# An account of every engine's clock in place of fixed waits: emission order in a two-layer hybrid decoder trunk

## The chip, the cores and the metric

The kernel runs on one core of one Trainium2 chip. The metric is the device time of one execution in microseconds (us), here the median of three runs. The engines are TensorE (PE, matrix products and transposes), VectorE (DVE), ScalarE (ACT), GpSimd (POOL) and SyncE (SP), whose queue issues nearly all transfers.

## The reference

The kernel computes two layers of a decoder trunk on 512 tokens of 1024 features, all in float32:

```python
for l in range(DEPTH):
    proj = rms_norm(h, norm_mix_pre[l]) @ w_in[l]
    (aq, ak, av, cb, cc, cx, gq, gk, gv, ga, gb, gg) = jnp.split(proj, split_idx, axis=-1)
    y_attn = dilated_attention_mixer(aq, ak, av, cos, sin)          # 4 heads of 64
    y_conv = short_conv_mixer(cb, cc, cx, conv_short[l])            # 256 channels
    y_gdn = gated_deltanet_mixer(gq, gk, gv, ga, gb, gg, ...)       # 4 heads of 128, chunked recurrence
    mix = jnp.concatenate([y_attn, y_conv, y_gdn], axis=-1) @ w_out[l]
    h = h + rms_norm(mix, norm_mix_post[l])
    xa = memory_cross_attention(rms_norm(h, norm_xattn_pre[l]), rms_norm(mem, norm_mem[l]), w_xq[l], w_xkv[l], w_xo[l])
    h = h + rms_norm(xa, norm_xattn_post[l])
    gate, up = jnp.split(rms_norm(h, norm_ffn_pre[l]) @ w_gate_up[l], 2, axis=-1)
    h = h + rms_norm((jax.nn.silu(gate) * up) @ w_down[l], norm_ffn_post[l])
```

The DeltaNet solves a triangular system per chunk and head, and carries a state from chunk to chunk; the kernel uses chunks of 128 tokens, four in all.

## The kernel before

**Bulk products.** The weight projections are products of float32 accuracy made of parts: each weight chunk (512 KB) is loaded into a raw tile, split by ACT into a rounded part `hi` (name ending in `_hi`) and by DVE into the rest `lo`, and each block takes three products (`mm3`, lines 207 to 209). The names are those of the columns: gk, gq, gv and gg (DeltaNet keys, queries, values, gate), aq and av (attention; ak is part of aq), cb and cx (convolution), wo (output projection), xk, xv, xq and xo (cross-attention), gu (feed-forward's gate and up), da and db (the halves of its down projection). A number behind the name is the token block (wo, xo, db) or column block.

**Dependent chains.** Between them stand small chains: a norm ahead of each sub-layer (`prenorm`: squares and sums on ACT, a power on POOL, the scaling on DVE into `mix_hn`, `xa_hn` or `ff_hn`, transposes on PE into `mix_pt`, `xa_pt` or `ff_pt`, and their split into `hT..._h` on ACT and `hT..._l` on DVE); the same for the memory (`mem_x`, `mem_pt`, `mT`); the norm and residual behind an output projection (`wo_z`, `wo_sq`, `wo0p_r`, then `h`; in the feed-forward `dacc`, `fsq`, `ffnp_r`); and the DeltaNet's chain. That one makes the decays: a product gives their running sums by columns and by rows (`dcol`, `drow`), DVE copies them (`dcol_s`, `drow_s`), SP stores drow_s to DRAM (`dD`) and loads it back on all partitions (`edrow`), ACT makes `relT` of it, and for each chunk DVE forms `A` from relT and the product `G` of the keys (`gk_c`). A goes through DRAM into a substitution and its inverse through DRAM again (`X`, `Z` from `dX`, `dZ`), then through products (`W1p`, `dZ`) to the recurrence. `fq` is a factor for the queries, from the sum of squares `gq_ss` by a power on POOL (`gq_r`).

**What sets the order.** All is one program that is emitted by tasks. A task is a Python generator; it emits some instructions and yields a wait in ns or the name of an event. `Driver.run` always continues the ready task of the lowest priority number; the bulk has 50, chains have less. `Driver.t` counts PE's time by fixed numbers, and a clock each for DVE and ACT says only when what they were given is done. A chain that needs PE yields `lag(extra)`: until DVE and ACT are through, 300 ns, and an extra that is set by hand for each place:

```python
        yield self.lag({"mix": 3000, "xa": 7000, "ff": 2500}[name])
```

`chunk(i)`, called by the bulk, loads up to chunk i + 3 and splits up to i + 2 at that moment. What is emitted is a priority: the framework then lists the instructions by it and by their dependences, and each engine runs its own list in order. Tiles come from rings of fixed numbers of buffers: 3 raw tiles, 5 each of hi and lo, and in the accumulator memory 3 banks for bulk, 3 ("g") and 2 ("a") for chains.

Nearly all instructions of DVE and ACT are recorded at line 122 (the helper `Engine`), transposes at 201, float32 products at 197, and POOL's powers at 228 and 595.

Of the kernel before, what the change touches and what calls it, by code (L numbers as in the profile page):

```python
# [26 lines left out]
# SBUF tiles of 2 KB, by stream: slots of a stream are given out in the order of emission  # L27
# [6 lines left out]
def shape_constants():  # L34
    """Identity, triangles, block and window masks, rotary frequencies: all from shapes alone."""
# [18 lines left out]
class Driver:  # L54
# [5 lines left out]
    def __init__(self):  # L60
        self.t = 0.0
        self.tasks = []
        self.events = {}
        self.n = 0
        self.engines = {"v": 0.0, "a": 0.0}

    def busy(self, engine, ns):
        self.engines[engine] = max(self.engines[engine], self.t) + ns
# [9 lines left out]
    def fire(self, event):  # L78
        self.events[event] = self.t + self.lag()

    def ready(self, task):
        if task[4] is not None:
            if task[4] not in self.events:
                return None
            task[3] = max(task[3], self.events[task[4]])
            task[4] = None
        return task[3]
# [22 lines left out]
class Engine:  # L110
    """An engine whose instructions are also counted on the driver's clock."""

    def __init__(self, engine, driver, name, fixed, per):
        self._e, self._d, self._n, self._f, self._p = engine, driver, name, fixed, per

    def __getattr__(self, op):
        f = getattr(self._e, op)

        def call(*args, **kw):
            n = max(math.prod(x.shape[1:]) for x in list(args) + list(kw.values()) if hasattr(x, "shape"))  # L120
            self._d.busy(self._n, self._f + self._p * n)
            return f(*args, **kw)  # L122
        return call


class Group:
    """One projection: columns of a weight against activations, feature- or token-major."""
# [22 lines left out]
class Trunk:  # L150
    AHEAD = 2

    def __init__(self, ctx, tc, T, out, dbg=None):
        self.tc, self.nc, self.T, self.out = tc, tc.nc, T, out
# [3 lines left out]
        self.raw_p = pool("raw", 3)  # L158
        self.w_p = pool("w", 5)
# [5 lines left out]
        self.dr = Driver()  # L165
        self.lag = self.dr.lag
        self.v = Engine(tc.nc.vector, self.dr, "v", 140, 1.0)
        self.a = Engine(tc.nc.scalar, self.dr, "a", 200, 0.83)
        self.groups = []
        self.loaded = []  # L170
        self.made = []

    def B(self, tag, name, shape=(128, 512), dt=F32):
        return self.b_p.tile(list(shape), dt, tag="b" + tag, name=name, bufs=SLOTS[tag])

    def T8(self, name, shape=(128, 4, 512), dt=F32):
        return self.t8_p.tile(list(shape), dt, tag="t8", name=name)

    def sm(self, name, w=16):
        return self.s_p.tile([128, w], F32, tag="sm%d" % w, name=name, bufs={32: 2, 16: 26}.get(w, 20))  # L180

    def ps(self, tag, name, shape=(128, 512)):
        return self.ps_p.tile(list(shape), F32, tag="ps" + tag, name=name, bufs=BANKS[tag])
# [5 lines left out]
    @staticmethod  # L189
    def later(wait, gen):  # L190
        yield wait
        yield from gen

# [1 line left out]
    def mm(self, out, a, b, start=True, stop=True):  # L195
        """float32 product of up to 128 columns."""
        self.nc.tensor.matmul(out, a, b, start=start, stop=stop)  # L197
        self.dr.t += 215.0 * max(128, out.shape[-1]) / 128

    def tr(self, out, src):  # L200
        self.nc.tensor.transpose(out, src, self.ident)  # L201
        self.dr.t += 215.0

    def mm3(self, out, wh, wl, xh, xl, first, last):
        """float32 product from parts of 12 bits: (wh + wl)^T (xh + xl)."""
# [4 lines left out]
        self.dr.t += 3 * max(107.0, out.shape[-1] / 2.37)  # L210

# [6 lines left out]
    def rsqrt(self, name, a, add, eps, mul=None):  # L218
        """(a + add + eps)^-0.5 or (a * mul + eps)^-0.5, per element."""
# [11 lines left out]
    def wbc(self, name, row, tag="e"):  # L231
        """A weight row on every partition, in two halves."""
# [8 lines left out]
    def load(self, upto):  # L241
        """Load and split weight chunks, in the order of their use."""
        nc = self.nc
        while len(self.loaded) <= upto and len(self.loaded) < len(self.order):
            g, (cols, ks) = self.order[len(self.loaded)]
            nk, width = len(ks), sum(n for _, n in cols)
            raw = self.raw_p.tile([128, 1024], F32, tag="raw", name=g.name + "_raw")
            rv = raw[:, :nk * width].rearrange("p (k n) -> p k n", k=nk)
            o = 0
            for c0, n in cols:  # L250
                src = g.w[ks[0] * 128:(ks[0] + nk) * 128, c0:c0 + n].rearrange("(k p) n -> p k n", p=128)
                nc.sync.dma_start(rv[:, :, o:o + n], src)
                o += n
            self.loaded.append((ks, raw, nk, width, g.name))

    def chunk(self, i):
        """(k tiles, hi, lo) of chunk i; the ones behind it are on their way."""
        self.load(i + self.AHEAD + 1)
        while len(self.made) <= min(i + self.AHEAD, len(self.order) - 1):
            ks, raw, nk, width, name = self.loaded[len(self.made)]  # L260
            hi = self.w_p.tile([128, 1024], F32R, tag="whi", name=name + "_hi")
            lo = self.w_p.tile([128, 1024], F32R, tag="wlo", name=name + "_lo")
            n = nk * width
            self.split(hi[:, :n], lo[:, :n], raw[:, :n])
            self.made.append((ks, hi[:, :n].rearrange("p (k n) -> p k n", k=nk),
                              lo[:, :n].rearrange("p (k n) -> p k n", k=nk)))
            self.loaded[len(self.made) - 1] = None
        return self.made[i]

    def bulk(self):  # L270
        base = 0
        for g in self.groups:
# [8 lines left out]
            for i in range(base, base + n):  # L281
                self.made[i] = None
            base += n

    def run_fm(self, g, base, need):
# [5 lines left out]
        per = len(g.kts) // 4 if len(g.kts) >= 4 else 1  # L291

# [9 lines left out]
        for hf, sl in enumerate(halves):  # L302
            if hf and len(need) > 1:
                yield need[1]
            for i in range(len(g.chunks)):
                ch = self.chunk(base + i)
                for n in range(i // per * 2, min(nt, i // per * 2 + 2)):
                    block(n, ch, sl)
                    if hf == len(halves) - 1 and i % per == per - 1:
                        g.evac(n, pts[n])  # L310
                    yield 0

    def run_tm(self, g, base, need):
# [5 lines left out]
        def block(tb, ch):  # L319
            ks, hi, lo = ch  # L320
            if pts[tb] is None:
                tag = "b" if first == 0 or tb < 3 else "g"
# [5 lines left out]
        for i in range(first):  # L328
            ch = self.chunk(base + i)
            for tb in range(g.ntb):  # L330
                if g.kneed:
                    for k in ch[0]:
                        yield g.kneed(k, tb)
                block(tb, ch)
                if i == n - 1:
                    g.evac(tb, pts[tb])
                yield 0
        if g.tb_outer:
            for tb in range(g.ntb):
                for i in range(first, n):  # L340
                    ch = self.chunk(base + i)
                    if g.kneed:
                        for k in ch[0]:
                            yield g.kneed(k, tb)
                    block(tb, ch)
                    yield 0
                g.evac(tb, pts[tb])

# [1 line left out]
    def transposed(self, name, src, dst_hi, dst_lo):  # L350
        """src: two [128 tok, 512]; (hi, lo) of its transpose for each group of 4 k tiles."""
# [9 lines left out]
    def prenorm(self, name, tb, wb, hT, event, spill=False):  # L361
# [8 lines left out]
        yield self.lag({"mix": 3000, "xa": 7000, "ff": 2500}[name])  # L370
# [52 lines left out]
    def h_tiles(self, src, tbs=range(NTB)):  # L423
        """The residual stream from DRAM: per token block two tiles of 512 features."""
# [21 lines left out]
    def setup2(self):  # L446
# [5 lines left out]
        for l in range(2):  # L452
# [3 lines left out]
            nc.sync.dma_start(rows[o + 54:o + 55, :], T["gdn_norm"][l:l + 1, :])  # L456
        pt = self.ps("g", "rows_pt", (128, 128))
# [15 lines left out]
        yield 25000.0  # L473
        # zeroed scratch around the diagonal blocks
        zero = self.B("r", "zero", (128, 4, 128))
        self.v.memset(zero, 0.0)
# [4 lines left out]
        self.dH = self.d_p.tile([S, D], F32, name="dH")  # L481
        for c in range(4):
            nc.sync.dma_start(self.full(self.dX, c), zero)
# [3 lines left out]
    def full(d, c):  # L487
        """The four heads' 128 x 128 matrices of a chunk in scratch."""
# [3 lines left out]
    def diag(d, i, j, n, m):  # L492
        """Of their 32 x 32 diagonal blocks, (chunk, head, block) in order, the n x m from row i and column j."""
# [838 lines left out]
```

## Time and profile before

| | |
|---|---|
| three runs, us | 1658.7, 1660.26, 1662.85 (median 1660.26) |
| the profiled execution | span 1660.5 us |
| instructions | 21539 |
| busy: PE, PE weight loads, DVE, ACT, POOL | 98%, 82%, 53%, 39%, 4% |
| granted clock of PE, mean | 0.996 |
| DMA | 174.56 MB, 105 GB/s on average |

The span is the time from the first instruction to the last of the profiled execution; here it stands 0.2 us above the median. The profile's waits put an engine's idle time down to what ended last ("PE G L197 <- DVE A" is PE idle ahead of a product into G until DVE had written A). Matmuls are pipelined, and the times of their ends overlap; start to start is the time that one takes.

### The profile page before, as it was taken

What the parts mean: (1) busy time and instruction counts of PE and PEld (TensorE: products, weight loads), DVE (VectorE), ACT (ScalarE), POOL (GpSimd) and SP (SyncE); (2) the same over time, 40 slices, a digit from 0 to 9 for tenths busy, and PEclk for the clock granted to TensorE, in tenths of its full rate; (3) what the DMA queues carried; (4) which work ended last, traced back from release to release, by engine and by line L of the source; (5) the groups of instructions that cost most, each with busy time, mean ns of one, the idle gap of its engine ahead of it and who ended that gap; (6) DMA issues with size and microseconds to landing.
All of it is one profiled execution on the core that took longest, in us unless ns stands there. A gap on an engine that the chain in (4) does not pass through costs nothing.

```text
span 1660.5 us, 21539 instructions
## 1 busy us (share of the span) xinstructions
PE 1619.2 (98%) x8457; PEld 1361.5 (82%) x8457; DVE 878.8 (53%) x1640; ACT 644.3 (39%) x1195; POOL 73.4 (4%) x76
## 2 busy tenths in 40 slices
PE   7999999999999999999999999999999999999998
PEld 6878777888888888888788778778888888888886
DVE  6979475745463332233489785667455533223334
ACT  5543344544343222332345443455344423223221
POOL 0010000100010000000000200000000100000000
PEclk9999999999999999999999999999999999999999
DMA  6445323442233323334333351425421332333331
GB/s 189 134 125 117 94 88 128 137 155 65 75 91 101 100 91 102 98 93 127 89 106 112 95 146 58 133 70 165 140 76 52 114 102 89 101 93 97 102 101 51
DMA packets 169201, 174.56 MB, mean 105 GB/s; under 512 B 29950, under 2 KB 132620, under 8 KB 169100
## 3 DMA queue, kind: packets, MB, share of 16 engines
q1 hardware_dynamic: 169100, 173.19, 34.6%
q8 instruction: 66, 1.08, 0.3%
q14 instruction: 35, 0.29, 0.1%
HBM read 163.71 MB, written 9.45 MB: 104 GB/s over the span
## 4 chain that ended last, share of the span: by engine, by line
PE 77%; DVE 11%; issue 3%; DMA 3%; POOL 3%; ACT 3%; SPq 0%; POOLq 0%; DVEq 0%; ACTq 0%
DVE h L122 1%; PE yp L197 1%; PE sc L197 1%; DMA Z<-dZ 1%; PE dZ L197 1%; PE O L197 1%; DMA edrow<-dD 1%; DVE gq_c L122 1%; PE W1p L197 1%; DVE X L122 1%; DVE xk_lo L122 1%; ACT junk L122 1%; DVE t L122 0%; POOL ff_r L228 0%; DVE xa_hn L122 0%
## 5 line engine op out<-in xcount | busy, mean ns | idle before, releaser
L122 DVE TENSOR_TENSOR gu_lo<-gu_raw,gu_hi 128x1024 fp32r<-128x1024 f32 x88 | 107.7, 1224 | 260.8 <-ACT gu_hi L122 260.8
L122 ACT ACTIVATE gu_hi<-gu_raw 128x1024 fp32r<-128x1024 f32 x88 | 93.1, 1060 | 228.4 <-issue 109.9
L122 DVE TENSOR_TENSOR da_lo<-da_raw,da_hi 128x1024 fp32r<-128x1024 f32 x24 | 29.4, 1225 | 83.1 <-ACT da_hi L122 83.1
L122 DVE TENSOR_TENSOR db_lo<-db_raw,db_hi 128x1024 fp32r<-128x1024 f32 x20 | 24.5, 1225 | 58.0 <-ACT db_hi L122 58.0
L122 ACT ACTIVATE da_hi<-da_raw 128x1024 fp32r<-128x1024 f32 x24 | 25.5, 1060 | 74.9 <-issue 23.7
L122 ACT ACTIVATE gh<-silu 128x512 fp32r<-128x512 f32 x44 | 27.2, 622 | 51.6 <-DVE silu L122 51.6
L122 ACT ACTIVATE db_hi<-db_raw 128x1024 fp32r<-128x1024 f32 x20 | 21.2, 1060 | 58.6 <-issue 23.7
L122 DVE TENSOR_TENSOR gl<-silu,gh 128x512 fp32r<-128x512 f32 x44 | 30.1, 688 | 14.2 <-ACT gh L122 14.2
L228 POOL TENSOR_TENSOR ffnp_r<-ffnp_t,nhalf 128x1 f32<-128x1 f32 x8 | 4.4, 548 | 707.3 <-DVE ffnp_t L122 707.3
L122 DVE TENSOR_TENSOR xq_lo<-xq_raw,xq_hi 128x1024 fp32r<-128x1024 f32 x16 | 19.6, 1226 | 24.3 <-ACT xq_hi L122 23.8
L122 ACT ACTIVATE P<-P,m 128x128 f32<-128x128 f32 (+3 forms) x32 | 17.9, 560 | 27.1 <-DVE m L122 25.8
L201 PE MATMUL mix_pt<-cst,mix_hn 128*128 128x128 f32 x64 | 13.1, 346 | 14.8 <-DVE mix_hn L122 13.3
L122 ACT ACTIVATE xq_hi<-xq_raw 128x1024 fp32r<-128x1024 f32 x16 | 17.0, 1061 | 23.9 <-DMA xq_raw<-in_w_xq 4.9
L122 DVE TENSOR_TENSOR xv_lo<-xv_raw,xv_hi 128x1024 fp32r<-128x1024 f32 x16 | 19.6, 1225 | 12.0 <-ACT xv_hi L122 11.5
L122 ACT ACTIVATE junk<-dacc 128x512 f32<-128x512 f32 x16 | 10.1, 629 | 39.4 <-DVE dacc L122 39.3
L122 ACT ACTIVATE xP<-xs,xm 128x256 f32<-128x256 f32 x32 | 14.9, 470 | 26.6 <-DVE xm L122 26.6
L201 PEld LDWEIGHTS mix_pt<-cst,mix_hn 128*128 128x128 f32 x64 | 9.0, 174 | 18.0 <-DVE mix_hn L122 12.0
L122 ACT ACTIVATE xk_hi<-xk_raw 128x1024 fp32r<-128x1024 f32 x16 | 16.9, 1057 | 14.3 <-DMA xk_raw<-in_w_xkv 13.0
L122 ACT ACTIVATE xv_hi<-xv_raw 128x1024 fp32r<-128x1024 f32 x16 | 17.0, 1060 | 14.1 <-DMA xv_raw<-in_w_xkv 4.8
L122 DVE TENSOR_TENSOR xk_lo<-xk_raw,xk_hi 128x1024 fp32r<-128x1024 f32 x16 | 19.3, 1216 | 3.7 <-ACT xk_hi L122 3.7
L197 PE MATMUL sc<-qkT,qkT 64*128 64x128 f32 (+3 forms) x64 | 20.6, 482 | 0.0
L122 DVE TENSOR_TENSOR X<-X,t 64x31 f32<-64x31 f32 (+30 forms) x62 | 19.3, 312 | 1.1
(2283 smaller groups left out, 5418.5 us busy)
## 6 DMA issues: line engine op xcount, KB each, us to landing
gu_raw<-in_w_gate_up SPq DMA_DIRECT2D x88, 512.0 KB, 3.5
da_raw<-in_w_down SPq DMA_DIRECT2D x24, 512.0 KB, 3.8
db_raw<-in_w_down SPq DMA_DIRECT2D x20, 512.0 KB, 3.8
xk_raw<-in_w_xkv SPq DMA_DIRECT2D x16, 512.0 KB, 3.6
xv_raw<-in_w_xkv SPq DMA_DIRECT2D x16, 512.0 KB, 4.6
xq_raw<-in_w_xq SPq DMA_DIRECT2D x16, 512.0 KB, 4.5
h<-in_x SPq DMA_DIRECT2D x16, 256.0 KB, 4.8
gk_raw<-in_w_in SPq DMA_DIRECT2D x8, 512.0 KB, 7.9
```

The source lines that it names most:

```text
L122: return f(*args, **kw)
L197: self.nc.tensor.matmul(out, a, b, start=start, stop=stop)
L201: self.nc.tensor.transpose(out, src, self.ident)
L228: nc.gpsimd.tensor_tensor(r, t, self.nhalf[:, :w], op=ALU.pow)
```

## The change

The driver keeps an account of all engines: clocks for DVE, ACT, POOL, SP and the transfers, gaps in the engines' clocks that later work may fill, and for each tile, in grains of 32 columns, when it was last written (and by which engine) and read. Each call of an engine goes through a wrapper that costs it by a formula and books it. A task's yield is now `when(tiles, bank=...)`: until the tiles named are written by the account, and until the oldest bank of that ring is free. All hand-set waits (4500, 800, 7000 and so on) go. The bulk asks the account for each block too.

```diff
-    def lag(self, extra=0.0):
-        """Until VectorE and ScalarE are through with what they have been given."""
-        return max(max(self.engines.values()) - self.t, 0.0) + 300.0 + extra
+    def when(self, *aps, slot=None):
+        t = self.t
+        for ap in aps:
+            st, gs = self.grains(ap)
+            for g in gs:
+                if g in st["w"]:
+                    t = max(t, st["w"][g][0] + self.SEM)
+        return max(t - self.t, self.slot(*slot) if slot else 0.0)
...
+    def pe(self, ns, out, ins):
+        start = self.begin("pe", self.t, [out], ins)
+        self.t = start + ns
+        self.end("pe", [out], ins, start + ns, start + ns + 180.0)
...
+    COST = {"v": (157.0, 1.04), "a": (175.0, 0.87), "g": (560.0, 1.5)}
...
     def fire(self, event):
-        self.events[event] = self.t + self.lag()
+        self.events.add(event)
...
-        yield self.lag({"mix": 3000, "xa": 7000, "ff": 2500}[name])
+        yield self.when(*hn, bank="g")
...
-            yield 4000.0
+            yield self.when(*x)
...
-            yield self.lag(1500)
+            yield self.when(*x, bank="g")
```

Weights are fed by a task of their own, of priority 49, which keeps the three raw tiles loading and splits a chunk once the account has it landed and one of the five pairs is free:

```diff
+    def feeder(self):
+        total = len(self.order)
+        while len(self.made) < total:
+            while len(self.loaded) < min(total, len(self.made) + self.RAWS):
+                self.load()
+            n = len(self.made)
+            if n < self.used + self.CHUNKS:
+                raw = self.loaded[n][1]
+                wait = self.when(raw[:, :self.loaded[n][2] * self.loaded[n][3]])
+                if wait <= 0.0:
+                    self.make()
+                    wait = 0.0
+                yield wait
+            else:
+                yield 200.0
...
     def chunk(self, i):
-        self.load(i + self.AHEAD + 1)
-        while len(self.made) <= min(i + self.AHEAD, len(self.order) - 1):
...
+        self.asked = i
+        while len(self.made) <= i:
+            while len(self.loaded) <= i:
+                self.load()
+            self.make()
         return self.made[i]
...
-        yield 25000.0
+        yield 60000.0
+
         zero = self.B("r", "zero", (128, 4, 128))
         self.v.memset(zero, 0.0)
         for c in range(4):
+            yield 4000.0
             nc.sync.dma_start(self.full(self.dX, c), zero)
             nc.sync.dma_start(self.full(self.dZ, c), zero)
```

The instructions are the same; their order is not. Three places follow, each on DVE (a row is line, operation, what it writes and reads, and the shape).

The decays in layer 0, before:

```order
L122 TENSOR_TENSOR g__930<-a__897,nea 128x16
L122 TENSOR_SCALAR gq_t<-gq_ss 32x16 x4
L122 SCALAR_TENSOR_TENSOR gv_c_998<-gv_t_1003,gv_c_998 128x512
L122 TENSOR_SCALAR fq<-gq_r 128x16
L122 COPY drow_s<-drow 16x128
L122 TENSOR_TENSOR fq_958<-fq 128x16
L122 COPY dcol_s<-dcol 128x16
```

and after:

```order
L245 TENSOR_TENSOR g__930<-a__897,nea 128x16
L245 COPY dcol_s<-dcol 128x16
L245 COPY drow_s<-drow 16x128
L245 TENSOR_SCALAR rkh<-gk_r 128x16
L245 SCALAR_TENSOR_TENSOR gv_c_1089<-gv_2__1043,vecs,gv_c_1089 128x511
```

The step on gq_ss and both on fq have moved to places ahead of these rows; the two copies follow g.

Output projection to cross-attention in layer 0, before:

```order
L122 TENSOR_TENSOR hTxa_l_2912<-xa_pt,hTxa_h_2910 128x4x128
L122 TENSOR_SCALAR xa_t<-xa_ss 128x1
L122 TENSOR_TENSOR xk_lo<-xk_raw,xk_hi 128x1024
L122 TENSOR_TENSOR hTxa_l_2913<-xa_pt,hTxa_h_2911 128x4x128
L122 SCALAR_TENSOR_TENSOR xa_hn<-h,xa_r,w_xa 128x512 x2
L122 TENSOR_TENSOR hTxa_l_2912<-xa_pt,hTxa_h_2910 128x4x128
L122 TENSOR_TENSOR hTxa_l_2913<-xa_pt,hTxa_h_2911 128x4x128
L122 TENSOR_TENSOR wo_z_3068<-wo0b__3004,w_mixpost 128x512
```

and after:

```order
L245 SCALAR_TENSOR_TENSOR xa_hn<-h,xa_r,w_xa 128x512 x2
L245 TENSOR_TENSOR hTxa_l_2884<-xa_pt,hTxa_h_2882 128x4x128
L245 TENSOR_TENSOR hTxa_l_2885<-xa_pt,hTxa_h_2883 128x4x128
L245 TENSOR_TENSOR mT_2658<-mem_pt,mT_2654 128x2x128
L245 TENSOR_TENSOR xk_lo<-xk_raw,xk_hi 128x1024
L245 TENSOR_TENSOR mT_2659<-mem_pt,mT_2655 128x2x128
L245 TENSOR_TENSOR mT_2660<-mem_pt,mT_2656 128x2x128
L245 TENSOR_TENSOR hTxa_l_2884<-xa_pt,hTxa_h_2882 128x4x128
L245 TENSOR_TENSOR mT_2661<-mem_pt,mT_2657 128x2x128
L245 TENSOR_TENSOR hTxa_l_2885<-xa_pt,hTxa_h_2883 128x4x128
L245 TENSOR_TENSOR wo_z_3098<-wo0b__3009,w_mixpost 128x512
```

The splits of the second memory block (mT) stood some twenty-five rows ahead of this place, and stand between those of the stream's second and third token blocks now.

The boundary of the layers, before:

```order
L122 TENSOR_TENSOR dacc<-db_2__6780,dacc 128x512
L122 TENSOR_TENSOR gk_lo<-gk_raw,gk_hi 128x1024
L122 TENSOR_TENSOR dacc<-dacc,w_fpost 128x512
L122 TENSOR_SCALAR ffnp_t<-fsq 128x1
L122 TENSOR_TENSOR hTmix_l_6857<-mix_pt,hTmix_h_6855 128x4x128
L122 SCALAR_TENSOR_TENSOR h<-dacc,ffnp_r,h 128x512 x2
L122 TENSOR_TENSOR hTmix_l_6858<-mix_pt,hTmix_h_6856 128x4x128
L122 TENSOR_TENSOR dacc<-db_3__6787,dacc 128x512
L122 TENSOR_SCALAR mix_t<-mix_ss 128x1
L122 TENSOR_TENSOR gk_lo<-gk_raw,gk_hi 128x1024
L122 SCALAR_TENSOR_TENSOR mix_hn<-h,mix_r,w_mix 128x512 x2
```

and after:

```order
L245 TENSOR_TENSOR dacc<-db_2__6796,dacc 128x512
L245 TENSOR_TENSOR gk_lo<-gk_raw,gk_hi 128x1024
L245 TENSOR_TENSOR dacc<-dacc,w_fpost 128x512
L245 TENSOR_SCALAR ffnp_t<-fsq 128x1
L245 TENSOR_TENSOR gk_lo<-gk_raw,gk_hi 128x1024
L245 SCALAR_TENSOR_TENSOR h<-dacc,ffnp_r,h 128x512 x2
L245 TENSOR_TENSOR gk_lo<-gk_raw,gk_hi 128x1024
L245 TENSOR_SCALAR mix_t<-mix_ss 128x1
L245 TENSOR_TENSOR dacc<-db_3__6803,dacc 128x512
L245 SCALAR_TENSOR_TENSOR mix_hn<-h,mix_r,w_mix 128x512 x2
```

Three splits of gk stand between db_2's product and the third block's mix_hn instead of two, and the splits of the second block's transposes (hTmix_l) stand behind it.

More of the change, by code (lines that the diff above doesn't have):

```diff
@@ new lines, in __init__, with put, slot, done @@
+        self.rings = {}
+        self.spans = {}
+    def put(self, tile, tag, n):
+        ring = self.rings.setdefault(tag, [])
+        name = tile.tensor.name
+        self.state[name] = {"before": ring[-n] if len(ring) >= n else None, "w": {}, "r": {}, "from": None}
+        ring.append(name)
+        return tile
+    def slot(self, tag, n):
+        ring = self.rings.get(tag, [])
+        return self.done(ring[-n]) + self.SEM - self.t if len(ring) >= n else 0.0
+    def done(self, name):
+        st = self.state[name]
+        return max([0.0] + [x for x, _ in st["w"].values()] + list(st["r"].values()))
@@ new lines, in grains @@
+    def grains(self, ap):
+        t = ap.tensor
+        name = t.name
+        if name not in self.state:
+            self.state[name] = {"before": None, "w": {}, "r": {}, "from": 0.0}
+        st = self.state[name]
+        if not on_chip(ap):
+            return st, (0,)
+        row = math.prod(t.shape[1:])
+        key = (ap.offset % row, tuple(tuple(x) for x in ap.ap[1:]))
+        if key not in self.spans:
+            idx = np.array([key[0]])
+            for step, count in key[1]:
+                idx = (idx[:, None] + step * np.arange(count)[None, :]).reshape(-1)
+            self.spans[key] = sorted(set((idx // self.GRAIN).tolist()))
+        return st, self.spans[key]
@@ new lines, in begin @@
+    def begin(self, engine, start, outs, ins):
+        for ap in ins:
+            st, gs = self.grains(ap)
+            for g in gs:
+                w = st["w"].get(g)
+                if w:
+                    start = max(start, w[0] + (self.SEM if w[1] != engine else 0.0))
+        for ap in outs:
+            st, gs = self.grains(ap)
+            if st["from"] is None:
+                st["from"] = self.done(st["before"]) + self.SEM if st["before"] else 0.0
+            start = max(start, st["from"])
+            for g in gs:
+                w = st["w"].get(g)
+                if w and w[1] != engine:
+                    start = max(start, w[0] + self.SEM)
+                start = max(start, st["r"].get(g, 0.0))
+        return start
@@ new lines, in pe, with dma @@
+    def pe(self, ns, out, ins):
+        start = self.begin("pe", self.t, [out], ins)
+        self.t = start + ns
+        self.end("pe", [out], ins, start + ns, start + ns + 180.0)
+    def dma(self, out, src):
+        start = self.begin("sp", self.free["sp"], [out], [src])
+        self.free["sp"] = start + 100.0
+        far = src if on_chip(out) else out
+        run = far.ap[-1][1] * 4 if far.ap[-1][0] == 1 else 4
+        rate = 230.0 if run > 512 else 120.0 if run == 512 else 60.0
+        moved = max(self.free["dma"], start + 100.0) + 4 * math.prod(out.shape) / rate
+        self.free["dma"] = moved
+        self.end("sp", [out], [src], moved, moved + 1700.0)
@@ L238, in wbc @@
         return t
[L241 to L254, printed above, removed]
@@ L291, in run_fm, with ready @@
         per = len(g.kts) // 4 if len(g.kts) >= 4 else 1
+        def ready(n, ch, sl):
+            ks, hi, lo = ch
+            aps = [x[:, :, c(n % 2)] for x in (hi, lo)] + [x[:, sl] for k in ks for x in g.act(k)]
+            tag = "a" if g.half and n == 3 else "b"
+            return self.when(*aps, bank=tag if pts[n] is None else None)
         def block(n, ch, sl):
@@ L317, in run_tm, with steps @@
         first = g.lead if g.tb_outer else n
-        def block(tb, ch):
-            ks, hi, lo = ch
+        def steps(tb, i):
+            ch = ks, hi, lo = self.chunk(base + i)
+            if g.kneed:
+                for k in ks:
+                    yield g.kneed(k, tb)
+            tag = "b" if first == 0 or tb < 3 else "g"
+            yield self.when(hi, lo, *[x for k in ks for x in g.act(k, tb)], bank=tag if pts[tb] is None else None)
             if pts[tb] is None:
-                tag = "b" if first == 0 or tb < 3 else "g"
                 pts[tb] = self.ps(tag, f"{g.name}_{tb}_", (128, g.width))
@@ L328, in run_tm @@
         for i in range(first):
-            ch = self.chunk(base + i)
             for tb in range(g.ntb):
[L331 to L334, printed above, removed]
+                yield from steps(tb, i)
                 if i == n - 1:
@@ L456, in setup2 @@
             nc.sync.dma_start(rows[o + 54:o + 55, :], T["gdn_norm"][l:l + 1, :])
+        yield self.when(rows, bank="g")
         pt = self.ps("g", "rows_pt", (128, 128))
@@ L583, in sumsq @@
                 yield 700.0
-            yield self.lag(1000)
+            yield self.when(part, bank="g")
             out = self.ps("g", pre + "_ss", (128, 64))
@@ L823, in queries @@
                 yield ev(f"rel{c}")
+                yield self.when(*qT, st["relT"][c], bank="a")
                 P = self.ps("a", "KQ", HT)
@@ L1146, in head @@
             for i in range(2):
+                yield self.when(*Ph, *Pl, bank=bank)
                 op = self.ps(bank, "xo_p")
```

263 lines of the change are left out of this document (171 added, 92 removed).

## The prediction

> **What bounds the kernel now.** I read the page's first part, then busy time by windows of 20 us, then the waits of TensorE, then the engines' time lines at each long wait. The page first.
>
> ```profile
> span 1660.5 us, 21539 instructions
> PE 1619.2 (98%) x8457; PEld 1361.5 (82%) x8457; DVE 878.8 (53%) x1640; ACT 644.3 (39%) x1195; POOL 73.4 (4%) x76
> ```
>
> TensorE (PE) is busy 1619.2 of 1660.5 us, so 41.3 us are all that an order of emission can win, less what no order reaches. Where they lie is told by the windows; the columns are busy time (instructions) of PE, weight loads, VectorE (DVE), ScalarE (ACT) and GpSimd (POOL), then the granted TensorE clock, the DMA share and the GB/s.
>
> ```profile
> 0.00:20.00 20.00, 7.91 (x31) 6.05 (x32) 9.59 (x18) 11.74 (x26) 3.32 (x8) 1.00 0.69 239
> 100.00:120.00 20.00, 16.98 (x96) 14.18 (x95) 14.06 (x46) 12.74 (x34) 2.61 (x3) 1.00 0.41 120
> 300.00:320.00 20.00, 19.64 (x159) 19.01 (x159) 19.18 (x29) 13.63 (x27) 3.35 (x3) 1.00 0.47 153
> 540.00:560.00 20.00, 20.00 (x90) 16.57 (x89) 6.04 (x8) 5.40 (x7) 0.00 (x0) 1.00 0.33 106
> 820.00:840.00 20.00, 17.99 (x92) 15.04 (x91) 14.40 (x24) 11.19 (x24) 3.47 (x5) 0.91 0.30 106
> 920.00:940.00 20.00, 16.88 (x85) 14.68 (x86) 13.63 (x43) 13.48 (x35) 1.27 (x2) 0.83 0.42 120
> 1640.00:1660.50 20.50, 12.78 (x57) 10.25 (x55) 9.77 (x17) 2.17 (x6) 1.64 (x3) 0.91 0.27 102
> ```
>
> The head (0 to 20) leaves 12.1 us idle and the tail (from 1640) 7.7 us; the feed-forward, of which 540 to 560 is a sample, leaves none. So 41.3 - 12.1 - 7.7 = 21.5 us idle lie in the middle, plus what a lower clock costs: (1 - 0.91) x 20 = 1.8 us at 820 and (1 - 0.83) x 20 = 3.4 us at 920. The new order has the first hundred rows of PE and the last thirty of every engine as they were, so I cost head and tail at nothing; they hang on DMA and on the last norm, which nothing else covers, and any shift there would count in full. The window at 300 shows the opposite of slack: PE is full, but DVE is busy 19.18 of 20 us too.
>
> The waits name the middle.
>
> ```profile
> PE mix_pt L201 <- DVE mix_hn L122: 13.3, 6, 8.3
> PE G L197 <- DVE A L122: 5.6, 2, 3.1
> PE ff_pt L201 <- DVE ff_hn L122: 4.4, 4, 1.5
> PE W1p L197 <- DMA Z<-dZ: 2.2, 4, 1.1
> PE xk__10118 L207 <- DVE Kl L122: 1.5, 1, 1.5
> PE G L197 <- DVE drow_s L122: 1.1, 2, 0.5
> PE xk__3339 L207 <- DVE Kl L122: 1.2, 1, 1.2
> PE av__808 L207 <- DVE gq_c L122: 1.0, 1, 1.0
> ```
>
> Each row gives the total, the number of waits and the longest; the 8.3 of mix_pt is the head.
>
> **The change, part by part.** No product, split or transfer is added or removed: the same instructions stand in another order, and PE's work summed by rows is the same. So every term is a wait that goes or comes, or a switch between kinds of products.
>
> (1) The decay chain of the DeltaNet, gain. The place in layer 0:
>
> ```profile
> 97.93 3.41 POOL L595 TENSOR_TENSOR gq_r<-gq_t,nhalf 128x16 f32<-128x16 f32 x1 [23.92 <-DVE gq_t L122]
> 101.37 0.17 DVE L122 TENSOR_SCALAR fq<-gq_r 128x16 f32<-128x16 f32 x1 [2.80 <-POOL gq_r L595]
> 101.57 0.28 DVE L122 COPY drow_s<-drow 16x128 f32<-16x128 f32 x1
> 101.88 0.33 SPq L664 DMA_DIRECT2D dD<-drow_s  x1
> 111.02 1.13 DVE L122 SCALAR_TENSOR_TENSOR A<-G,cb,relT 128x128 f32<-128x128 f32 x4 [1.96 <-ACT relT L122]
> 112.20 1.16 PE L197 MATMUL G<-gk_c 128*128 128x128 f32 x8 [2.50 <-DVE A L122]
> 930.71 2.07 PE L197 MATMUL G<-gk_c 128*128 128x128 f32 x8 [3.12 <-DVE A L122]
> ```
>
> DVE holds fq ahead of drow_s, and fq waits 2.80 us for POOL's power; drow_s starts the DMA round trip that ends in relT and A, and the fourth G waits for A to free its bank (three banks). In the new order fq stands far earlier and drow_s follows the gate directly. The chain starts 2.8 + 0.2 = 3.0 us sooner, and by a count of PE's rows 11.5 us of products lie between drow and the fourth G instead of 10.5. Both waits on A (5.6) and both on drow_s (1.1) should go: -6.7. The lower clock at 920 follows the 3.12 us wait, and goes with it: -3.4. Against it stands SP's queue: in layer 0 the new order puts two weight loads and a zeroing write directly ahead of dD, and a load whose buffer is not free blocks what is behind it. I take no cost; bounds for the whole term: -10.1 (all goes) to -3 (half of the waits stays and the clock still drops once).
>
> (2) The inverse, gain: W1p waits four times for Z to come back by DMA, 2.2 in all. In the new order 18 to 20 us more PE work stands ahead of W1p in each layer (the attention's products): -2.2, bounds 0 and -2.2. The wait of av_0 for a bank, 1.0, should go as its chain is emitted later: -1.0, bounds 0 and -1.0.
>
> (3) Output projection to cross-attention, loss, once a layer. Before, both memory blocks are normalised and transposed 30 us earlier, and each norm of the stream is held back a fixed 7000 ns more. Now the second memory block comes between the stream's norms. Its price on DVE is two mem_x and four mT: 2 x 750 + 4 x 422 ns = 3.2 us.
>
> ```profile
> L122 DVE SCALAR_TENSOR_TENSOR mem_x<-mem_x,mem_r,w_mem 128x512 f32<-128x512 f32 x8 | 5.7, 750 | 2.2 <-POOL mem_r L228 2.2
> L122 DVE TENSOR_TENSOR mT<-mem_pt,mT 128x256 fp32r<-128x256 f32 x16 | 6.6, 422 | 3.0 <-ACT mT L122 2.9
> 301.70 1.21 DVE L122 TENSOR_TENSOR xk_lo<-xk_raw,xk_hi 128x1024 fp32r<-128x1024 f32 x1
> 303.43 1.40 DVE L122 SCALAR_TENSOR_TENSOR xa_hn<-h,xa_r,w_xa 128x512 f32<-128x512 f32 x2
> 304.75 1.28 DVE L122 TENSOR_TENSOR hTxa_l<-xa_pt,hTxa_h 128x512 fp32r<-128x512 f32 x2
> ```
>
> DVE has 0.8 us free there, so the 3.2 push the chain. From the last wo0b block of the third token block to the first full run of xk, PE has about 4.6 us of products (6 of wo0b, 14 of xk, 16 transposes), while DVE walks mem_x 1.5, hTxa_l 1.3, h 1.4, two xk_lo 2.4, xa_hn 1.4, another hTxa_l pair 1.3 and the first mT 0.4 = 9.7 us, of which it enters some 2 ahead. Walked row by row that leaves two gaps, 3.0 us and 1.9, and 0.7 in single switches: +5.6. The later waits on Kl (1.2 and 1.5, and two of 0.3 to 0.4) go: -1.7 a layer. Net +3.9 a layer, +7.8. Bounds: -3.4 for both (only the Kl waits go) to +11.2 (they stay elsewhere).
>
> (4) Layer boundary, loss, once.
>
> ```profile
> 830.47 1.75 PE L201 MATMUL mix_pt<-cst,mix_hn 128*128 128x128 f32 x8 [2.01 <-DVE mix_hn L122]
> 830.90 0.68 DVE L122 TENSOR_TENSOR dacc<-db__6780,dacc 128x512 f32<-128x512 f32 x1
> 831.50 1.22 DVE L122 TENSOR_TENSOR gk_lo<-gk_raw,gk_hi 128x1024 fp32r<-128x1024 f32 x1
> 834.17 1.41 DVE L122 SCALAR_TENSOR_TENSOR h<-dacc,ffnp_r,h 128x512 f32<-128x512 f32 x2
> 837.01 0.61 ACT L122 ACTIVATE mix_hn<-h 128x512 f32<-128x512 f32 x1
> 840.15 1.42 DVE L122 SCALAR_TENSOR_TENSOR mix_hn<-h,mix_r,w_mix 128x512 f32<-128x512 f32 x2 [0.44 <-POOL mix_r L228]
> ```
>
> The second token block's transposes are moved behind db_3, so their 2.01 us goes. But three gk_lo (1.22 each) now stand on DVE ahead of the third block's mix_hn instead of two. From the end of db_2 its chain is dacc 0.7, gk_lo 1.2, dacc 0.7, gk_lo 1.2, h 1.4, two squares with their sums on ACT 1.5, POOL 0.7, mix_hn 1.4, with the rest and hand-overs about 12.2 us; PE has db_3 (24 x 0.227 = 5.4), eight transposes (0.8) and four gk (0.5) = 6.7. Wait 5.5 instead of 2.0, some of it recovered behind: +3.0. Bounds -2 (no new wait) to +6. The 1.8 us of lower clock stays.
>
> (5) Cross-attention to feed-forward: the four ff_pt waits (4.4) become one wait a layer of about 2.4 for hTff_l behind two splits, and 0.3 each for the transposes: (2.7 x 2) - 4.4 = +1.0, bounds -1 and +2.
>
> (6) Recurrence and switches. The recurrence's steps now follow each other as soon as the account has their tiles, with short stretches of one projection (cb) between. I take 1.5 us for the last transposes of its output in layer 0, which have 2.7 us of work ahead of them and a chain of about 4.2 (four squares with their sums on ACT, with the hand-overs about 2.6; POOL 0.7; the product with gi on DVE 0.7, and its hand-over), and 1.0 elsewhere.
>
> ```profile
> L122 ACT ACTIVATE on<-O x32: 258/277/287, 199.4 to 1057.2; 128x128 f32<-128x128 f32 x32
> L122 ACT ACTIVATION_READ_ACCUMULATOR on<-O x32: 194/204/222, 199.5 to 1057.4; 128x1 f32 x32
> L122 DVE TENSOR_TENSOR on<-O,gi x8: 677/686/693, 202.8 to 1059.5; 128x512 f32<-128x512 f32 x8
> ```
>
> There are 39 more changes between kinds of products on PE (971 runs of one product instead of 932, counted in the two orders). What one costs:
>
> ```profile
> 113.20 1.06 PE L197 MATMUL KQ<-gq_c,gk_c 128*128 128x128 f32 x8
> 114.01 0.48 PE L209 MATMUL aq__1227<-aq_hi,hT_l 128*128 128x512 f32 x1
> 114.33 0.39 PE L207 MATMUL aq__1227<-aq_hi,hT_h 128*128 128x512 f32 x1
> 114.56 0.39 PE L208 MATMUL aq__1227<-aq_lo,hT_h 128*128 128x512 f32 x1
> ```
>
> The first product behind a switch holds PE 0.32 us from start to start, the next 0.23: 0.09 us. For 39 that is at most 3.5; many of the new switches are between products of one kind, so I take 2.0. Together +4.5, bounds 0 and +8.
>
> Weight feeding by itself I cost at nothing: in the feed-forward DVE is busy 6.04 of 20 us and PE never waits, so a split may stand some microseconds earlier or later there. If that cover failed (a split emitted too late), each of the feed-forward's chunks could stall PE by a split, 1.2 us; nothing in the order suggests it, since up to five chunks are split ahead of use instead of three.
>
> Sum: -10.1 - 2.2 - 1.0 + 7.8 + 3.0 + 1.0 + 4.5 = +3.0. On the profiled execution's 1660.5 us that gives 1663.5; the median of the runs shown is 0.2 lower, 1660.26, so I say **1663**.
>
> [...] The row first: half a microsecond after the 2.01 us wait at 830 a stretch of lower clock begins (0.91 over its window), but the 2.50 us wait at 112 lowers nothing (its window shows 1.00). [...]
>
> **The rivals.**
> A, my forecast: gains of (1) and (2) against losses of (3), (4) and (6). Speaks for it: the gains have rows, the losses are on stretches where DVE is nearly full. Against: the losses are walked by hand.
> B, faster: the gaps of (3) and (4) don't open, because ACT and DVE run far enough ahead of PE there (only 1.5 of 20 us of PE are gone at any such place before). Then (3) is -3.4, (4) is 0: -13.3 - 3.4 + 0 + 1.0 + 4.5 = -11.2, so 1649. For it: each of these chains is shorter than the 20 us window, and the windows have an average of 53% DVE. Against it: 19.18 of 20 us at 300. It decides when DVE enters the place 3 us earlier than I take.
> C, slower: each of the four new gaps of (3) and one more in (4) pulls the clock down, at 1.8 us (the price of the window at 820): 5 x 1.8 = 9 on top of A, 1672. For it: 820 and 920. Against it: 112. It decides at a gap of about 2 to 3 us that lies badly.
> D, the change does nothing that counts: the waits of (1) go but come back as waits on the DMA round trip (SP's queue), and the hand-overs stay as they are; -3 and +3, 1660. For it: the round trip is still the longest part of that chain. Against it: the 2.80 us on fq are plainly in front of it.
>
> **How the numbers follow.** Chances: A 0.42, B 0.30, C 0.18, D 0.10. A's own range is 1656 to 1670: the bounds of (3) by half, of (4) and of (6). The range for 8 in 10 reaches from B's 1649 less 2 for (6) to C's 1672 plus 2: 1647 to 1674. With 0.3% (5 us) as what a measurement here can tell, faster means under 1655.3 and slower over 1665.2. B is faster, with a twentieth of A: 0.33. C and a third of A are slower: 0.33. D and the rest are the same: 0.34.
>
> **What would show it.** (1) fq ahead of g on DVE with no wait on POOL behind the gate, no wait of G on A, and 1.00 granted around 920. (2) No wait of W1p on Z. (3) Waits of mem_pt or xk on mT or hTxa_l around 300 and 1130 of 1.5 to 3 us each, and DVE at 19 of 20 or more there. (4) One wait of mix_pt around 830 to 840, of about 5 us, and none of 2.0 before it. (5) Two waits of gu on hTff_l. (6) PE's busy time up by 2 to 4 us with the same instructions. I am wrong if (3) and (4) leave no idle time on PE (B), if the granted clock falls in new windows (C), or if the feed-forward's windows are no longer full, for which I have no term.

## The result: slower, beyond the range

The changed kernel took 1678.35 us (median of four runs, 1676.18 to 1678.94) against 1661.55 for the kernel before in the same sitting: ratio 1.0101, 95% interval 1.0089 to 1.0113. The forecast was 1663, with a range of 1647 to 1674. The profiled execution spans 1677.2 us, 16.7 more than before; the gaps below are read in it. First the page's head and the windows (columns as in the prediction); the last fence has four of the same windows in the kernel before.

```profile
span 1677.2 us, 21526 instructions
PE 1629.1 (97%) x8457; PEld 1368.4 (82%) x8457; DVE 881.1 (53%) x1640; ACT 646.0 (39%) x1195; POOL 67.0 (4%) x76
```

```profile
100.00:120.00 20.00, 20.00 (x114) 17.34 (x114) 17.70 (x60) 13.93 (x38) 1.92 (x3) 1.00 0.55 159
200.00:220.00 20.00, 19.66 (x127) 14.02 (x127) 10.00 (x34) 7.95 (x22) 0.00 (x0) 0.91 0.26 79
240.00:260.00 20.00, 17.35 (x113) 14.75 (x112) 14.30 (x39) 7.81 (x24) 2.84 (x3) 1.00 0.33 106
300.00:320.00 20.00, 17.11 (x117) 15.19 (x116) 18.85 (x31) 13.28 (x27) 3.49 (x4) 0.91 0.34 108
460.00:480.00 20.00, 18.45 (x100) 15.96 (x99) 16.45 (x27) 11.10 (x24) 3.59 (x5) 0.91 0.25 73
840.00:860.00 20.00, 13.09 (x86) 12.24 (x85) 15.88 (x25) 9.76 (x21) 3.07 (x4) 0.74 0.52 158
920.00:940.00 20.00, 18.38 (x94) 15.14 (x93) 17.69 (x44) 9.77 (x20) 0.00 (x0) 1.00 0.59 167
1120.00:1140.00 20.00, 15.73 (x81) 13.13 (x80) 16.55 (x30) 12.77 (x29) 3.65 (x5) 0.94 0.16 53
```

```profile
200.00:220.00 20.00, 19.66 (x133) 16.66 (x132) 15.17 (x45) 9.44 (x28) 2.02 (x2) 1.00 0.10 28
240.00:260.00 20.00, 20.00 (x99) 14.36 (x98) 10.41 (x25) 8.29 (x22) 0.56 (x1) 1.00 0.56 176
840.00:860.00 20.00, 19.33 (x160) 18.73 (x159) 14.08 (x21) 7.71 (x13) 2.06 (x3) 1.00 0.43 126
1120.00:1140.00 20.00, 19.74 (x157) 18.96 (x156) 19.27 (x30) 13.82 (x27) 3.34 (x3) 1.00 0.44 139
```

Of the places of the decay chain, the one at 100 is filled, as forecast; the one at 920 is fuller (18.38 instead of 16.88), what is left there is a new wait of 1.6 us, and its clock is back at 1.00. New holes stand at the recurrence (240), at the hand-overs (300, 840, 1120), and between head and tail the clock is lowered, to 0.50, in six places instead of two (27.3 us in all instead of 10.2). PE's busy time grew by 9.9 us with the same products, its idle time by the rest, 6.8. The waits of PE tell the same:

```profile
PE mix_pt L245 <- DVE mix_hn L245: 13.6, 4, 7.8
PE mem_pt L245 <- DVE hTxa_l L245: 6.6, 4, 2.6
PE oT L245 <- DVE on L245: 3.9, 4, 1.0
PE gk__7072 L245 <- ACT hTmix_h L245: 2.4, 1, 2.4
PE dcol L245 <- DVE g__7719 L245: 1.6, 1, 1.6
PE gu__4576 L245 <- ACT hTff_h L245: 1.3, 2, 1.0
PE V L245 <- DVE vsc L245: 1.3, 2, 0.6
PE dcol L245 <- DVE g__930 L245: 1.1, 1, 1.1
```

To account for all of it, I took PE's products from start to start and subtracted what each shape takes where PE never waits (227 ns for 512 columns, 120 for 256, about 110 for a float32 product or transpose of 128). What is left is lost time, whatever its form: a wait, a slow clock, a switch. Cut at landmarks of the program (us lost in each stage; the last columns are experiments, told below):

| stage | before | after | price (e5) | early (e14) | both (e16) |
|---|---|---|---|---|---|
| head | 9.1 | 8.9 | 7.9 | 7.6 | 8.9 |
| layer 0: DeltaNet's front, to the first scores | 5.7 | 2.8 | 3.8 | 3.0 | 3.7 |
| to the first W1p | 1.7 | 1.9 | 2.3 | 2.2 | 2.4 |
| inverse, recurrence, to wo0b | 7.4 | 13.5 | 5.0 | 11.1 | 5.0 |
| wo0b to cross-attention | 2.1 | 5.9 | 7.2 | 4.2 | 4.2 |
| to feed-forward | 2.6 | 4.0 | 2.5 | 1.0 | 1.0 |
| layer boundary | 5.2 | 10.2 | 9.6 | 4.5 | 4.2 |
| layer 1: front | 8.0 | 3.4 | 3.4 | 5.1 | 4.8 |
| to the first W1p | 0.9 | 2.3 | 2.3 | 2.4 | 2.4 |
| inverse, recurrence, to wo1b | 7.6 | 8.7 | 5.0 | 8.7 | 5.2 |
| wo1b to cross-attention | 2.4 | 7.3 | 7.3 | 5.1 | 5.0 |
| to feed-forward | 2.6 | 4.0 | 4.0 | 1.0 | 1.0 |
| all (with stages that lose under 1) | 56.8 | 74.0 | 61.5 | 55.5 | 47.4 |

The table is good to about a microsecond: from the start of the first product to that of the last the changed kernel takes 16.1 us more (1660.2 against 1644.1), where the stages add up to 17.2, and the level of a row depends on the prices taken for small shapes. Counted by form instead, some 5 us are products slowed by the halved clock (4.5 to 9.9), 7 to 8 are single waits over 0.4 us, and about 4 are switches and small change.

### The profile page after: what moved, and what is told of

Its sections match the earlier page's. It is cut to its first block, busy times and chain, and to the rows that moved or that the text cites. A ratio compares the mean times of both kernels' runs of the same rounds, so it can differ in the third digit from the quotient of the medians.

```text
span 1677.2 us, 21526 instructions
## 1 busy us (share of the span) xinstructions
PE 1629.1 (97%) x8457; PEld 1368.4 (82%) x8457; DVE 881.1 (53%) x1640; ACT 646.0 (39%) x1195; POOL 67.0 (4%) x76
## 4 chain that ended last, share of the span: by engine, by line
PE 81%; DVE 11%; ACT 3%; issue 2%; POOL 2%; DMA 1%; SPq 0%; POOLq 0%; DVEq 0%; ACTq 0%
PE xs L245 1%; PE xo_p L245 1%; PE sc L245 1%; PE yp L245 1%; DVE h L245 1%; PE dZ L245 1%; DVE gq_c L245 1%; PE W1p L245 1%; PE PT L245 1%; DVE gv_c L245 1%; DVE aq_lo L245 1%; PE da__12526 L245 0%; PE da__12519 L245 0%; PE da__12512 L245 0%; PE da__12499 L245 0%
## 5 line engine op out<-in xcount | busy, mean ns | idle before, releaser
L245 ACT ACTIVATE junk<-dacc 128x512 f32<-128x512 f32 x16 | 10.1, 628 | 39.8 <-DVE dacc L245 39.8
L245 ACT ACTIVATE PTs<-PT 128x128 f32<-128x128 f32 (+3 forms) x32 | 13.9, 434 | 20.9 <-PE PT L245 20.9
```

## The experiments

All ratios are against the kernel before, run on the same chip beside the experiment. The changed kernel itself was run in the first sitting alone, so what an experiment gains on it is taken from its 1678.35 (ratio 1.0101); the medians of the kernel before differ by 0.9 us from sitting to sitting.

**Loads when a tile is free (e1).** The recurrence was late: the substitution (first step on D) began at 136.0 instead of 128.1, W1p at 189.0 instead of 175.8, the first V at 225.3 instead of 194.6. On SP's queue two of the three loads of D stood behind weight loads. Before, then in the changed kernel:

```profile
124.09 0.69 SPq L717 DMA_DIRECT2D D<-dA  x1
126.30 1.31 SPq L720 DMA_DIRECT2D D<-dA  x2
128.09 0.19 DVE L122 TENSOR_TENSOR t<-D,X 64x31 f32<-64x31 f32 x1
194.64 1.06 PE L197 MATMUL V<-vsc,Z 128*128 128x128 f32 x8
```

```profile
120.33 0.69 SPq L245 DMA_DIRECT2D D<-dA  x1
130.62 0.59 SPq L245 DMA_DIRECT2D D<-dA  x1
133.33 0.58 SPq L245 DMA_DIRECT2D D<-dA  x1
135.96 0.19 DVE L245 TENSOR_TENSOR t<-D,X 64x31 f32<-64x31 f32 x1
189.01 1.28 PE L245 MATMUL W1p<-Z,Q 128*128 128x128 f32 x10
225.27 1.06 PE L245 MATMUL V<-vsc,Z 128*128 128x128 f32 x8
```

```diff
             while len(self.loaded) < min(total, len(self.made) + self.RAWS):
+                if self.dr.slot("raw", self.RAWS) > 0.0:
+                    break
                 self.load()
...
-                yield wait
+                yield min(wait, 200.0)
```

> The feeder issues a weight load only when the account has a raw tile free, so that no load stands blocked in SP's queue ahead of the DeltaNet's own transfers. Theory Q (queue): in layer 0 of the changed kernel the loads of D (issued at 120.3, 130.6, 133.3 us) and a store of dZ (176.0) stand behind weight loads that wait for a tile; the substitution starts 7 us late, W1p 13 us late, the bulk products that filled the recurrence's waits are used up before it, and the second memory block is pushed into the next hand-over. Q expects the substitution at 130 or earlier instead of 136.0, W1p at 180 or earlier instead of 189.0, the waits of mem_pt on hTxa_l (6.6 us) gone, and 8 to 14 us less than the changed kernel (1664 to 1670). Theory E (eager requests without margins): the waits come from chains that ask for PE the moment the account has their tiles; E expects 0 to 3 us less.

Measured 1670.56, ratio 1.0059 (1.0036 to 1.0083); three of the four runs lie within 0.3 us, the fourth took 1677.74. The three loads now left together, yet the substitution was no earlier:

```profile
119.28 2.89 SPq L245 DMA_DIRECT2D D<-dA  x3
135.62 0.19 DVE L245 TENSOR_TENSOR t<-D,X 64x31 f32<-64x31 f32 x1
```

So theory Q fell on its own point: the queue was crowded, but not what the substitution waited for. About half of the 8 us lies in the recurrence of layer 0 all the same: W1p is no earlier (190.3), but the first V starts at 217.8. Why is not shown; a store of dZ, which Q had named too, leaves at 173.3 instead of 176.0. The rest lies at the hand-overs: both memory blocks now stand ahead of them, the mem_pt waits on hTxa_l are gone (xk waits 2.1 us for Kl in each layer in their place), and three of the six lowered clocks are gone too (mean granted clock of the profiled execution 0.994, in the changed kernel 0.991).

**Attention kept for the recurrence (e2).**

```diff
             yield from pair_attention(0)
+            yield ev("inv0")
             yield from pair_attention(1)
```

> The second head pair of the attention waits for the inverse's first chunk (inv0), so that its products are left as filler beside the recurrence; loads and all other requests are as in the changed kernel. If the recurrence is slow for lack of filler, whatever made it late, the waits of oT and V (3.9 and 1.3 us) shrink by half or more and the time falls by 3 to 6 us, with the substitution still at 136 and W1p at 188 or 189. Theory E expects the waits to stay, since the requests are as eager as before: 0 to 2 us less. Neither expects the hand-overs (mem_pt 6.6, mix_pt) to change.

1670.71, ratio 1.0050 (1.0035 to 1.0065): 7.6 less, more than forecast. The substitution stayed at 135.1 and W1p at 188.1, and of the 3.9 us on oT 0.9 is left. Counted from start to start, nearly all of the gain (some 7 us) lies between the first W1p and wo0b of layer 0. So the recurrence lacked filler, whatever made it late. The mem_pt waits stayed, at 8.0.

**The old extras at the norms (e3).**

```diff
-        yield self.when(*hn, bank="g")
+        yield self.when(*hn, bank="g") + {"mix": 3000, "xa": 7000, "ff": 2500}[name]
```

> The fixed extras of the kernel before (mix 3000, xa 7000, ff 2500 ns) are added again to the norms' requests, on top of the account. Theory E expects the waits at the norm hand-overs (mix_pt in the middle 5.8, gk on hTmix_h 2.4, mem_pt 6.6, gu 3.6) to shrink to less than half: 6 to 10 us less than the changed kernel. Theory Q expects the layer boundary and the feed-forward hand-over to gain at most 3 us, and mem_pt to stay, since the memory is late for another reason.

1684.78, ratio 1.0131 (1.0113 to 1.0148): 6 us worse. Both theories missed. Later requests leave still less behind the transposes; xk then waits 3.0 us for mT and 2.4 for wo_z, and ff_pt 5.9 in two waits. That turned the question round: are the requests too late rather than too early?

**The old extras in the recurrence (e4).** 1000 ns ahead of V, 500 ahead of dS, 3000 ahead of oT.

> The recurrence's extras of the kernel before (1000 ns ahead of V, 500 ahead of dS, 3000 ahead of oT) are added again. Theory E expects the waits of oT and V (5.2 us) to go: 4 to 6 us less than the changed kernel. Theory Q, by which there is simply too little other work left beside the recurrence, expects at most 2 us less: the requests come later but the filler runs out all the same.

1669.39, ratio 1.0041 (1.0026 to 1.0056): 9 less, more than E said. The recurrence itself gave 2.5 us in layer 0 (13.5 to 11.0) and 1.2 in layer 1, and oT waits only 0.2 us. The rest is at the hand-overs behind it and in the clock, where three of the six lowered stretches are gone (mean granted clock 0.994 instead of 0.991). That part I can't assign by this run.

**The price of transfers (e5).** In e1 the data of D were there by about 126 (issue to landing 3.3 us) and the step was emitted for ten microseconds later. The account moves runs of 512 bytes at 120 bytes per ns and shorter ones at 60, one transfer behind the other.

```diff
-        rate = 230.0 if run > 512 else 120.0 if run == 512 else 60.0
+        rate = 230.0
```

> The account prices transfers of short runs like long ones (230 bytes per ns in place of 120 and 60); nothing else is changed. Theory Q fell in part: with the loads out of the way the substitution still began at 135.6 us, ten microseconds after its data landed. Theory P (price) says that the account takes the DeltaNet's trips through DRAM to be some 8 us longer each than they are (A stored to D back: 8 us in the trace), so that the steps behind them are emitted late, and the bulk products that should cover the recurrence are used up. P expects the substitution at 130 or earlier, W1p at 182 or earlier (189.0), waits of oT and V (5.2) to fall by half, and 4 to 9 us less than the changed kernel. If the price does not matter: within 2 us, substitution at 135 to 136.

1666.55, ratio 1.0033 (1.0020 to 1.0046): 11.8 less, beyond what P forecast. The substitution begins at 125.1, W1p in layer 0 at 184.5 (forecast 182 or less), the first V at 209.9; oT and V no longer wait. The recurrence's stages lose 5.0 each instead of 13.5 and 8.7, less than before the change, and no other stage of the table gained more than 1.6. This is shown: the overpriced round trips made the recurrence late, and PE had used up the projection (cx) and the attention that once lay beside it. Of the 96 products of cx in layer 0, 47 stood behind the first W1p before the change, none in the changed kernel, and 24 in this run.

```profile
119.23 2.84 SPq L245 DMA_DIRECT2D D<-dA  x3
125.08 0.19 DVE L245 TENSOR_TENSOR t<-D,X 64x31 f32<-64x31 f32 x1
184.46 1.06 PE L245 MATMUL W1p<-Z,Q 128*128 128x128 f32 x8
```

**Three chunks ahead (e6).** `if n < self.used + 3:` in the feeder in place of CHUNKS.

> The feeder splits at most three chunks ahead of the one in use instead of five, as the kernel before did. Theory F (feed) says that splits far ahead of use stand on DVE and ACT in front of the norms at the hand-overs (three gk_lo ahead of mix_hn at the layer boundary). F expects the waits of mix_pt and gk at the layer boundary (8.3 us in all without the head) to fall below 4 and the 10.2 us of half clock there to shrink to 3.4, and 5 to 9 us less than the changed kernel. If the splits are not what is late there: within 3 us, and waits of PE on the splits themselves may appear.

1671.47, ratio 1.0061 (1.0045 to 1.0077): 7 less, within F's range, but only half for F's reason. The wait of mix_pt on the third block fell away, while gk waits 2.4 and 2.2 for hTmix, 4.6 in all, and the slow clock there lasts 6.8 us instead of 10.2. The slow clock was forecast at 3.4. So splits far ahead cost something at the boundary, and do not explain it.

**Four edits together (e8).** e1, e4, e5 and e6.

> Four edits together: loads only when a raw tile is free, the transfer price of e5, the recurrence's extras of e4, and feeding three chunks ahead as in e6. By P and F together the substitution begins by 130, W1p by 180, both inverse pairs run without attention between, and projections (cx) are left beside the recurrence; the gain on the decay chain (8 us) stays. That gives 1650 to 1658, below both kernels. If the losses are not of these causes, it stays at 1663 or above.

1662.04, ratio 1.0002 (0.9991 to 1.0014): the forecast missed by 4 us. The recurrence was as wished (W1p at 174.4), but new waits came: 2.8 of dcol on g, and up to 2.3 of xa_pt on xa_hn; and the clock was still lowered six times (mean granted clock 0.992). Waits of xa_pt on xa_hn had grown with feeding at three alone (2.5 in e6 instead of 0.8), which points at that edit, but no run here takes it out of the four by itself.

**The norms asked earlier (e14).**

```diff
-        yield self.when(*hn, bank="g")
+        yield max(self.when(*hn, bank="g") - 1500.0, 0.0)
```

> The changed kernel, but the norms' transposes are requested 1500 ns before the account has their input ready, instead of exactly then. Theory G (greedy) says that at the hand-overs of norms PE first runs all products that are ready and then meets the transposes with nothing left to cover their split; asking earlier costs a wait of up to 1.5 us at the transposes but leaves db_3, wo0b or xo0b blocks behind them. G expects the waits of gk, gu and mix_pt at the layer boundary and the feed-forward (12.9 us, without the head) to fall to 8 or less, the half clock at the layer boundary from 10.2 us to 3.4, and 3 to 6 us less than the changed kernel. If the hand-overs are only late by DVE's queue: within 2 us, the waits change their names.

1660.63, ratio 0.9997 (0.9988 to 1.0006): 17.7 less, three times what G said. What was wrong is seen at the layer boundary of the changed kernel:

```profile
839.44 1.03 PE L245 MATMUL mix_pt<-cst,mix_hn 128*128 128x128 f32 x8
842.83 0.39 PE L245 MATMUL gk__7072<-hTmix_h,gk_hi 128*128 128x256 f32 x1 [2.35 <-ACT hTmix_h L245]
847.26 1.11 PE L245 MATMUL mix_pt<-cst,mix_hn 128*128 128x128 f32 x4 [3.69 <-DVE mix_hn L245]
849.24 1.11 PE L245 MATMUL mix_pt<-cst,mix_hn 128*128 128x128 f32 x4 [0.87 <-DVE hTmix_l L245]
```

The account runs all of db_3 before the transposes, exactly as long as they are not ready; then gk needs their split and nothing is left to cover it. Asked 1.5 us earlier, twelve db_3 products stay behind the transposes:

```profile
820.00:840.00 20.00, 17.07 (x99) 14.27 (x97) 16.59 (x27) 10.52 (x21) 4.48 (x5) 1.00 0.39 120
840.00:860.00 20.00, 19.75 (x164) 19.32 (x163) 13.31 (x20) 8.90 (x16) 1.10 (x2) 1.00 0.29 89
```

The boundary loses 4.5 us instead of 10.2, though gk still waits 2.1 for hTmix_l; each feed-forward hand-over loses 1.0 instead of 4.0, and in the whole middle the clock is never lowered (mean granted clock 0.999). G's size was short since it counted the clock at the layer boundary alone: 9.9 of the gain are products no longer slowed.

**The decay chain alone (e13).** The kernel before with one line, which puts fq behind drow_s:

```diff
         def queries():
+            yield ev("vs")
             yield self.lag()
```

> The kernel before with one edit: the queries' chain starts when the decays are out (event vs), so that fq and its wait for POOL stand behind drow_s on DVE; nothing of the account or the feeder. By the prediction's term (1) this alone takes the waits of G (6.7 us) and the half clock at 930 (6.8 us long, 3.4 lost): 1650 to 1655. If the gain of the changed kernel at that place has another cause: within 2 us of the kernel before. The attention and the inverse get other neighbours by it, which may cost or give 2 us.

1659.78, ratio 0.9991 (0.9980 to 1.0002): no difference that can be told. The waits of G on A and on drow_s went, and so did the half clock at 930 (one of 3.4 us came at 128; mean granted clock 0.998); drow_s is copied at 94.3 instead of 101.6. In their place KQ, whose later groups the edit pushed some 10 us back, waits for relT, and the recurrence for its output's norm:

```profile
PE KQ L197 <- DVE relT L122: 4.9, 2, 2.5
...
PE oT L201 <- DVE on L122: 2.9, 4, 1.3
```

So taking these waits away is not a gain by itself. What else in the new order makes the front stages of the changed kernel lose less, no run here isolates.

**Both causes (e16) and with e1 and e4 on top (e15).**

> Only two edits on the changed kernel: the transfer price of e5 and the norms 1500 ns early of e14. If the two causes are separate, price for the inverse and the recurrence and greed for the hand-overs, their gains add up: 11.8 and 17.7 us less than 1678 give 1649 (1647 to 1653), with the recurrence of layer 0 losing 5 to 7 us instead of 13.5 and the layer boundary about 5 instead of 10. If both were one cause seen twice, 1658 to 1661. The loads when free and the recurrence's margins of e15 would then be worth at most 3 us.

> The changed kernel with the transfer price of e5, loads only when a tile is free (e1), the recurrence's extras (e4) and the norms 1500 ns early (e14); five chunks ahead, as in the changed kernel. By P and G together: recurrence beside attention and cx as in the kernel before, both memory blocks ahead of the hand-over, decay chain without waits: 1650 to 1657. If it is above 1662, the account costs something that these four edits do not reach.

e16, with the two edits of e5 and e14: 1651.79, ratio 0.9943 (0.9931 to 0.9955). e15, with all four: 1651.69, ratio 0.9938 (0.9925 to 0.9952). Both beat both kernels; e1 and e4 add nothing that can be told to the two. The gains of e5 (11.8) and e14 (17.7) sum to 29.5, and the two together give 26.6: nearly separate causes, as the table's last columns show stage by stage.

```profile
span 1649.8 us, 21534 instructions
PE 1616.1 (98%) x8457; PEld 1357.8 (82%) x8457; DVE 879.1 (53%) x1640; ACT 644.3 (39%) x1195; POOL 65.6 (4%) x76
```

## Why the prediction was wrong, step by step

- **(1) Decay chain**, -10.1, and av_0 of (2), -1.0: the two front stages gave 2.9 and 4.6, -7.5. The waits of G and the lowered clock at 920 went as forecast. Not foreseen: dcol now waits for g (1.1 and 1.6), in layer 0 a weight split (aq_lo, 1.22 us) now stands on DVE right ahead of the step that makes g; for layer 1 the cause is left open.
- **(2) Inverse and (6) recurrence**, together +2.3 (-2.2 and +4.5, all switches counted here): the four stages gave +0.2, +6.1, +1.4 and +1.1 = +8.8. This is the step that failed, in its sign for (2) and in its size for (6), which had 2.5 us of waits in it. "18 to 20 us more PE work stands ahead of W1p" was read as a gain of 2.2 us; it was the sign that the whole chain is late and that the recurrence's cover is spent. I saw cb as "short stretches between" and did not ask where cx had gone; e5 and e2 show that it is this cover which was missing.
- **(3) Cross-attention**, +7.8: +8.7. The waits are where they were placed (mem_pt on hTxa_l, 6.6 us in four waits, forecast as gaps of 3.0 and 1.9 in each layer); they are shorter than forecast, and a lowered clock in each layer (0.50 for 3.4 us from 304.6 and from 1137.5), which the sum had left out, makes up the size. So the near agreement is in part luck.
- **(4) Layer boundary**, +3.0: +5.0. The wait for the third block (5.5 forecast) was 3.7 + 0.9; the 2.35 us of gk on hTmix_h was not in the sum, and the clock, taken as unchanged at 0.91, fell to 0.74.
- **(5) Feed-forward**, +1.0: +2.8, again with a lowered clock in each layer (0.50 for 3.4 us from 475.3 and from 1304.7).
- **The rivals.** C came true in part: five new stretches of half clock and a longer one at the boundary, about 5 us more (9 forecast). C stood on top of A, at 1672, and the range ended 2 us above it; with what the recurrence cost beyond its terms, 6.5 us, the time lies beyond that. B failed since the gaps did open. D failed since the hand-overs did not stay as they were; its premise, SP's queue, is in the trace, but clearing it (e1) brought the substitution no earlier. (The chances add up to 0.32 faster, 0.32 slower and 0.36 the same; nothing hangs on the difference.)
- **The sum**: +3.0 forecast, +17.2 by stages. Weight feeding at no cost held for the feed-forward.

## To carry to other kernels

An account that asks for an engine at the very moment its input is ready spends all cover beforehand; what comes behind the step (here the split of a transpose) needs cover too, so ask a little early and accept a short wait. A wrong price in such an account does not show as a wait at the step that is priced, but as missing cover much later: compare when data land with when the step on them was placed. And where a lowered clock follows a gap, the price is the gap and the slow products behind it together: at the layer boundary of the changed kernel PE waited 2.35 us for hTmix_h, and 10.2 us at 0.50 followed, with starts of products of 256 columns 0.21 us apart where they are 0.12 at full clock.

## What the runs showed of the hardware

**When the clock was lowered.** Between head and tail the granted clock stands at 0.50, in the profiled execution of the changed kernel, for 3.4 us each from 202.2, 304.6, 475.3, 1137.5 and 1304.7 and for 10.2 us from 843.9; in that of the kernel before, for 3.4 us from 830.9 and for 6.8 us from 929.9. All the rest of the middle shows 1.00.

**What it costs.** In the changed kernel the products of 512 columns into wo0b start 0.23 us apart at 300, and 0.43 at 305, in a lowered stretch; those of 256 columns into gk 0.12 apart at 855, and 0.21 at 851, in another.

**What stands ahead of it.** The length of a wait alone does not tell whether a lowered stretch follows. In the kernel before one began right behind the 2.01 us wait at 830, and none behind the 2.50 us wait at 112; PE was busy 1.99 us of the four from 826.9 to 830.9, and 1.50 us of the four from 108.5 to 112.5. In the changed kernel PE was busy 3.76 of the four us ahead of 202.2, and the clock fell there all the same. What brings it down, no run here isolates.
